# Odd layer: output projection of six heads under the last head pair, with weights and gate prepared earlier

## The chip, the cores and the metric

One Trainium2 chip, one of its cores. The metric is the device time of one execution in microseconds (us). The engines are TensorE (PE; its weight loads are PEld), VectorE (DVE), ScalarE (ACT), GpSimd (POOL) and SyncE (SP), which issues the DMA transfers here.

## The reference, cut to what matters

Two layers run over 512 latent tokens (and, in the even layer, 256 context tokens) of width 1024. Layer 0 has a mixer of delta-rule and retention heads; layer 1, the odd one, has differential attention with 8 heads. Each layer has a mixer and a convolutional feed-forward net; each adds its gated result to the scaled stream and normalizes.

```python
def diff_mix(q, k, v, lam):
    s = jnp.einsum('cbhqd,cbhkd->cbhqk', q, k).astype(jnp.float32) * DIFF_HD ** -0.5
    p = jax.nn.softmax(s, -1)
    a = p[0] - lam * p[1]
    return jnp.einsum('bhqk,bhkd->bhqd', a.astype(v.dtype), v)
...
    def finish(o):
        o = rms_norm(o) * subln_w.astype(f32) * (1.0 - lambda_init)
        return (merge_heads(o).astype(w_out.dtype) @ w_out).astype(h.dtype)
```

The mixer's result y (512x1024) goes into layer_norm(alpha * x + gate * y), with alpha the DeepNorm constant; x is itself the normalized output of the stage before, times ln_g plus ln_b. A gate is a row of 1024 numbers. A matrix product in float32 is computed as three products of high and low parts: a tile is split into a rounded high part (hi) and the rest (lo), and hi*hi, hi*lo and lo*hi are added in PSUM.

## The kernel before, in words

Tokens stand in four tiles of 128 (t = 0 to 3). A weight unit is 256 columns of a 1024-row matrix: `unit` (L174) loads 1 MB into a tile `raw`, multiplies it by a gate row on POOL where one is given (L185), and `split` (L139) writes the high part on ACT (L147, tiles `whi`) and the low part on DVE or POOL (L148, `wlo`); `lo_engs` says which, "v" or "g".

`odd_mixer` (L1540) goes through the 8 heads in four pairs. `attend` (L1649) computes one head tile by tile: scores `sc` on PE, their maximum on DVE (L1663), exp on ACT (L1666), the difference of the two softmaxes on DVE (L1674), transposes and the product with the values on PE (`aT_ps`), copies (L1682), the head's output into `oall` (L1686) and its square sum (L1687). After four tiles the head's norm runs on DVE: a Newton iteration on 128x4 values (L1693, L127 to L136) and four scalings of `oall` (L1696). Between two tiles `attend` yields, and the loop over the pairs takes a few steps of a generator `fill`. In pairs 0 to 2 `fill` is `project` (L1604), which makes keys, queries and values of the next pair; its key and query tiles pass a rotary step (`rope`: products on DVE at L1577 and L1581, sum on POOL at L1583), transposes on PE (`oT_ps`) and evictions on ACT and DVE (L1591 to L1595).

In the last pair (pr == 3) `fill` is `sums` (L1708). At its start the four units of the output matrix are issued: 0 and 1 unscaled and split on DVE, 2 and 3 multiplied by the gate and split on POOL. `sums` transposes a head (`to_y`, L1700: `yT_ps` on PE, high part on ACT at L1705, low part on DVE at L1706) and accumulates its product with units 0 and 1, columns 0 to 511, for the token tiles 0 and 1, which hold the two PSUM banks of the pool `pj`. After the attention come tiles 2 and 3, heads 6 and 7 and then `out_proj_ln` (L1299): the stream is loaded and multiplied by ln_g on DVE and added to ln_b on POOL (`load_x`, L1324, L1325, both rows scaled by alpha at L1317), columns 0 to 511 are multiplied by the gate (L1346) and added (L1347), columns 512 to 1023 are computed and added (L1349), the statistics and the normalization follow (L1220 to L1240), and `h_tiles` (L1265) transposes the result and makes the high and low parts `hTh`, `hTl` for the feed-forward net.

The order on each engine is made when the program is built: a scheduler takes instructions by priority, which is the order in the code moved by `priority(offset)` (L155), so that what is marked with `LATE` (200, L47) may fall behind. At run time each engine takes its own list in order and waits where data or a buffer isn't there.

## Time and profile before

| | us |
|---|---|
| median of three runs | 2075.88 (2069.97 to 2078.63) |
| profiled execution, its own time | 2078.59 |
| its span | 2076.8 |
| PE busy | 1944.0 (94%) |
| DVE busy | 1246.6 (60%) |
| POOL busy | 776.1 (37%) |
| ACT busy | 716.3 (34%) |

The share of PE is a mean over the whole program; the part that the change touches lies between about 1500 and 1700 us of the span. All times below count from the start of the span. In rows of the order of time a row gives the start, the busy time, engine, line, operation, output and inputs; the bracket at the end is the idle time of the engine before it and what ended it.

### The profile page before, as it was taken

The page shows a single profiled execution, that of the slowest core. Times are in us where ns is not written, and L with a number is a line of the kernel's source. Part 1 is how long each engine was busy: PE and PEld are TensorE (multiplying, and loading weights), DVE is VectorE, ACT ScalarE, POOL GpSimd, SP SyncE. Part 2 cuts the span into 40 slices and gives each one's busy share as a digit, 9 for nine tenths or more (in the row PEclk, how much of TensorE's full clock was granted, in tenths as well). Part 3 has the DMA queues.
Part 4 walks back from the last instruction along what each step waited for, and adds up shares of the span by engine and source line. Part 5 has one row for each costly group of instructions (what it writes and reads, how often), then busy time and mean ns, then how long its engine had stood idle before and what let it go on. Part 6 is the DMA issues. An engine that isn't in the chain of part 4 may idle for free. (4 is left out here: it accounts for less than half of the span.)

```text
span 2076.8 us, 33472 instructions
## 1 busy us (share of the span) xinstructions
PE 1944.0 (94%) x13766; PEld 1671.6 (80%) x13766; DVE 1246.6 (60%) x2446; ACT 716.3 (34%) x1252; POOL 776.1 (37%) x412
## 2 busy tenths in 40 slices
PE   6989999999899999999999998999997989999997
PEld 4877777778888988888888886989886887888886
DVE  2354645533466685666666558366667687756567
ACT  2331332522334432222222225354554443323221
POOL 1233223222322244554554434122213126766572
PEclk8999999999999999999999999999999999999999
DMA  8546344455614231111111112010102133233221
GB/s 254 176 124 173 113 132 133 139 159 182 188 53 163 82 102 62 61 61 61 62 61 61 61 61 89 21 42 27 56 32 86 68 131 113 83 100 101 82 81 41
DMA packets 195585, 201.33 MB, mean 97 GB/s; under 512 B 21112, under 2 KB 183512, under 8 KB 195432
## 3 DMA queue, kind: packets, MB, share of 16 engines
q1 hardware_dynamic: 194136, 197.57, 30.4%
q8 instruction: 108, 1.77, 0.4%
q10 hardware_dynamic: 1296, 1.62, 0.2%
q14 instruction: 45, 0.37, 0.1%
HBM read 185.89 MB, written 13.27 MB: 96 GB/s over the span
## 5 line engine op out<-in xcount | busy, mean ns | idle before, releaser
L148 POOL TENSOR_TENSOR wlo<-raw,whi 128x2048 fp32r<-128x2048 f32 (+2 forms) x154 | 413.4, 2709 | 482.4 <-ACT whi L147 454.5
L1442 DVE SCALAR_TENSOR_TENSOR ac<-g_ps,fconvT,ac 128x441 f32<-128x441 f32 (+2 forms) x352 | 243.7, 694 | 191.0 <-ACT ac L1431 181.3
L147 ACT CAST whi<-raw 128x2048 fp32r<-128x2048 f32 (+2 forms) x177 | 200.3, 1169 | 379.7 <-PE d_ps L115 162.9
L115 PE MATMUL d_ps<-whi,hh 128*128 128x512 f32 x440 | 176.4, 401 | 11.4 <-DVE gt L1391 6.6
L115 PE MATMUL d_ps<-whi,hl 128*128 128x512 f32 x440 | 172.6, 392 | 0.6 <-DVE hl L148 0.6
L115 PE MATMUL d_ps<-wlo,hh 128*128 128x512 f32 x440 | 173.0, 393 | 0.0
L115 PE MATMUL opj<-whi,hTh 128*128 128x256 f32 x512 | 146.6, 286 | 2.1 <-ACT oq L1594 1.6
L115 PE MATMUL g_ps<-hTl,whi 128*128 128x512 f32 (+1 forms) x384 | 145.1, 378 | 2.9 <-POOL hTl L148 2.9
L115 PE MATMUL opj<-whi,hTl 128*128 128x256 f32 x512 | 145.2, 284 | 0.0
L115 PE MATMUL u_ps<-hTh,whi 128*128 128x512 f32 (+1 forms) x384 | 144.7, 377 | 0.0
L115 PE MATMUL opj<-wlo,hTh 128*128 128x256 f32 x512 | 144.6, 282 | 0.0
L115 PE MATMUL u_ps<-hTh,wlo 128*128 128x512 f32 (+1 forms) x384 | 144.6, 377 | 0.0
L115 PE MATMUL u_ps<-hTl,whi 128*128 128x512 f32 (+1 forms) x384 | 144.6, 376 | 0.0
L115 PE MATMUL g_ps<-hTh,whi 128*128 128x512 f32 (+1 forms) x384 | 144.5, 376 | 0.0
L115 PE MATMUL g_ps<-hTh,wlo 128*128 128x512 f32 (+1 forms) x384 | 144.2, 376 | 0.0
L115 PE MATMUL fpj<-whi,hTh 128*128 128x256 f32 x432 | 127.2, 295 | 5.8 <-DVE kT L550 4.7
L115 PE MATMUL fpj<-wlo,hTh 128*128 128x256 f32 x432 | 127.3, 295 | 0.0
L115 PE MATMUL fpj<-whi,hTl 128*128 128x256 f32 x432 | 126.3, 292 | 0.0
L115 PEld LDWEIGHTS d_ps<-whi,hh 128*128 128x128 f32 x440 | 83.1, 189 | 38.7 <-DVE gt L1391 17.0
L115 PEld LDWEIGHTS opj<-whi,hTh 128*128 128x128 f32 x512 | 97.2, 190 | 4.2 <-ACT oq L1594 2.6
L115 PE MATMUL c_ps<-hTh,wlo 128*128 128x256 f32 x352 | 98.9, 281 | 0.0
L115 PE MATMUL c_ps<-hTh,whi 128*128 128x256 f32 x352 | 98.8, 281 | 0.0
(462 smaller groups left out, 5011.2 us busy)
## 6 DMA issues: line engine op xcount, KB each, us to landing
mraw<-in_mod_w_dram SPq DMA_DIRECT2D x80, 512.0 KB
raw<-in_f_w_gate_dram SPq DMA_DIRECT2D x22, 1024.0 KB
raw<-in_f_w_up_dram SPq DMA_DIRECT2D x22, 1024.0 KB
raw<-in_f_w_down_dram SPq DMA_DIRECT2D x22, 1024.0 KB
raw<-in_o_w_qkv_dram SPq DMA_DIRECT2D x12, 1024.0 KB
raw<-in_e_w_in_dram SPq DMA_DIRECT2D x10, 1024.0 KB
mraw<-in_mod_w_dram SPq DMA_DIRECT2D x32, 256.0 KB
raw<-in_e_w_in_dram SPq DMA_DIRECT2D x12, 512.0 KB
```

Source lines behind the costliest of these rows:

```text
L115: self.nc.tensor.matmul(out, lhsT=lhsT, rhs=rhs, start=start, stop=stop)
L147: self.nc.scalar.copy(h, r)
L148: lo_eng.tensor_sub(l, r, h.bitcast(F32))
L1442: v.scalar_tensor_tensor(out=o, in0=pv[:, r0 + di:r1 + di, c0 + dj:c1 + dj], scalar=cw[(di + 1) * 3 + dj + 1], in1=o, op0=ALU.mult, op1=AL ...
```

## The change

- The gate row is loaded and summed in two halves of 512 columns (`half_gate`): the first in pair 1, the second at the start of the last pair.
- All four output units are multiplied by the gate and split on POOL. Unit 0 is issued in pair 2 after its sixth attention step, units 1 to 3 at the start of the last pair.
- `oall` now lies in the memory of the tile that the layer norm works in. After the heads 0 to 5 have been transposed, all at the start of the last pair, alpha * (x * ln_g + ln_b) is written over their 768 columns; the last 256 columns of it stand in a tile `rest`. The scaling of ln_g and ln_b by alpha is one ACT operation on both rows.
- `early` is the new `fill` of the last pair: the product of heads 0 to 5 for all four token tiles and both halves of the columns (288 of the 384 matmuls), each result added into the stream by DVE. The loop takes two steps of it per attention step, before one.
- After the attention heads 6 and 7 are transposed, their product (96 matmuls) is computed and added tile by tile, and the layer norm follows. The separate product with the gate is gone.
- `out_proj_ln` keeps the even layer's part alone.

```diff
-                def sums(accs, heads, late=0):
-                    for h in heads:
-                        to_y(h)
-                        with self.priority(late):
-                            self.out_part(accs, us[0], h, h == DHEADS - 1)
-                        yield
+                def early(heads):
+
+                    for n in range(2):
+                        for t in range(NLT):
+                            ps = pj.tile([P, 512], F32, tag="wo", name="wo_ps")
+                            with self.priority(LATE):
+                                for h in heads:
+                                    self.out_part([(t, ps)], us[n], h, h == heads[-1])
+                                    if h == heads[len(heads) // 2 - 1]:
+                                        yield
+                                for o, c0, n_ in rest(t, n):
+                                    v.tensor_add(o, ps[:, c0:c0 + n_], o)
+                            yield
...
+                def out_unit():
+                    sl = slice(len(us) * 256, (len(us) + 1) * 256)
+                    us.append(self.unit([w_out[:, sl]], gates[len(us) // 2][:, (len(us) % 2) * 256:][:, :256]))
+
+                def half_gate(pool, n, gb):
+
+                    t = pool.tile([P, 512], F32, name=f"gate{n}")
+                    nc.sync.dma_start(out=t, in_=self.gd[1][0][0][n * 512:(n + 1) * 512].partition_broadcast(P))
+                    nc.sync.dma_start(out=gb, in_=a["mod_b"][1, 2 * D + n * 512:2 * D + (n + 1) * 512]
+                                      .partition_broadcast(P))
+                    g.tensor_add(t, t, gb)
+                    gates.append(t)
+
                 for pr in range(4):
                     cur, nxt = nxt, {}
                     if pr < 3:
                         fill = project(pr + 1, ((4, 0, 2),), nxt)
+                        if pr == 1:
+                            half_gate(cpl, 0, self.rawp.tile([P, 8 * 256], F32, tag="raw", name="raw")[:, :512])
                     else:
                         stp.close()
-                        us = []
-                        self.lo_engs = "v"
-                        for u in range(4):
-                            if u == 2:
-                                self.lo_engs = "g"
-                                gate = self.gate_rows(self.pool(st, "gate1"), 1, 0, 1)[0]
-                                self.wps = [self.pool(st, "wout1", bufs=2)]
-                            sl = slice(u * 256, (u + 1) * 256)
-                            us.append(self.unit([w_out[:, sl]], gate[:, sl] if u > 1 else None))
+                        for h in range(6):
+                            to_y(h)
...
+                        half_gate(gatep, 1, end[:, 0:2, :].rearrange("p t n -> p (t n)"))
+                        out_unit()
+                        rows = self.rawp.tile([P, 8 * 256], F32, tag="raw", name="raw")
+                        for i, r in enumerate(("ln_g", "ln_b")):
+                            nc.sync.dma_start(out=rows[:, i * D:(i + 1) * D], in_=a[r][0, 1].partition_broadcast(P))
+                        s_.activation(rows, rows, AF.Copy, scale=ALPHA)
+                        for t in range(NLT):
+                            for o, c0 in ((oall[:, t, 0:768], 0), (end[:, t, :], 768)):
+                                cs = slice(c0, c0 + o.shape[1])
+                                nc.sync.dma_start(out=o, in_=self.x_src(2, t)[:, cs])
+                                v.tensor_mul(o, o, rows[:, cs])
+                                g.tensor_add(o, o, rows[:, D + c0:D + c0 + o.shape[1]])
+                        self.wps = [self.pool(st, "wout1", bufs=2)]
+                        out_unit()
+                        out_unit()
                         us = [us[:2], us[2:]]
                         self.lo_engs = "g"
-                        accs = [(t, pj.tile([P, 512], F32, tag="wo", name="wo_ps")) for t in range(2)]
-                        fill = sums(accs, range(6), LATE)
+                        fill = early(range(6))
+                    done = 0
...
-                                for _ in range(3 if pr < 3 else 1):
+                                for _ in range(3 if pr < 3 else 2):
                                     next(fill, None)
+                            done += 1
+                            if pr == 2 and done == 6:
+                                out_unit()
                     for _ in fill:
                         pass
+                for h in (6, 7):
+                    to_y(h)
...
+                for grp in ((0, 1), (2, 3)):
+                    sts = {t: self.ln_stats() for t in grp}
+                    for t in grp:
+                        for n in range(2):
+                            ps = po.tile([P, 512], F32, tag="wo", name="wo_ps")
+                            for h in (6, 7):
+                                self.out_part([(t, ps)], us[n], h, h == 7, first=6)
+                            for o, c0, n_ in rest(t, n):
+                                v.tensor_add(acc[t][:, n * 512 + c0:n * 512 + c0 + n_], ps[:, c0:c0 + n_], o)
+                            self.ln_half(acc[t], sts[t], n)
+                        self.ln_tile(acc[t], sts[t], acc[t], None)
+                    with self.priority(100):
+                        self.h_tiles("f1", grp, [acc[t] for t in grp])
```

POOL in pairs 2 and 3, before. L1583 is a rotary sum, L148 a low part of a weight unit, L1198 the sum of the gate row, L185 a gate product, L1325 the sum with ln_b in the tail.

```order
204 L148 TENSOR_TENSOR wlo<-raw,whi 128x2048
205 L1583 TENSOR_TENSOR otok<-otok,ob 128x512 x2
206 L148 TENSOR_TENSOR wlo<-raw,whi 128x2048 x2
207 L1583 TENSOR_TENSOR otok<-otok,ob 128x512 x2
208 L148 TENSOR_TENSOR wlo<-raw,whi 128x2048
209 L1583 TENSOR_TENSOR otok<-otok,ob 128x512 x2
210 L1198 TENSOR_TENSOR gate_15517<-gate_15517,raw 128x1024
211 L185 TENSOR_TENSOR raw<-raw,gate_15517 128x2048 x2
212 L148 TENSOR_TENSOR wlo<-raw,whi 128x2048 x2
213 L1325 TENSOR_TENSOR lx<-lx,lnb 128x1024 x4
```

The same place on POOL, changed. L1557 is the rotary sum (L1583 before), L1718 the sum of the second half gate, L1752 the sum with ln_b.

```order
208 L185 TENSOR_TENSOR raw<-raw,gate_13772 128x2048
209 L1557 TENSOR_TENSOR otok<-otok,ob 128x512 x2
210 L148 TENSOR_TENSOR wlo<-raw,whi 128x2048
211 L185 TENSOR_TENSOR raw<-raw,gate_13772 128x2048
212 L1557 TENSOR_TENSOR otok<-otok,ob 128x512 x2
213 L148 TENSOR_TENSOR wlo<-raw,whi 128x2048 x2
214 L1718 TENSOR_TENSOR gate_15561<-gate_15561,rest 128x512
215 L185 TENSOR_TENSOR raw<-raw,gate_15561 128x2048
216 L1752 TENSOR_TENSOR rest<-rest,raw 128x256 x3
217 L148 TENSOR_TENSOR wlo<-raw,whi 128x2048
218 L1752 TENSOR_TENSOR rest<-rest,raw 128x256
```

The gate product of unit 0 stands ahead of the two key sums of pair 2, that of unit 1 ahead of the two query sums (row 212); the splits of both units follow behind (row 213), and two more gate operations and the residual sums stand among the units of the last pair.

ACT in the second half of pair 2, before: L1591 to L1595 evict queries, L1638 copies values, L1666 is the exp.

```order
732 L1687 ACTIVATE pt,oss<-oall 128x128
733 L1594 ACTIVATE oq<-oT_ps 64x2x256
734 L1595 CAST oq<-oq 64x2x256
735 L1638 COPY ov<-opj 128x512
736 L1666 ACTIVATE sc,oZ<-sc,mx 128x768
737 L1682 COPY aT<-aT_ps 128x512
```

The same place on ACT, changed: L1746 scales both layer-norm rows, L1612 copies values, L1565 to L1569 evict queries, L1640 is the exp.

```order
732 L1565 ACTIVATE oq<-oT_ps 64x2x256
733 L1612 COPY ov<-opj 128x512
734 L1746 ACTIVATE raw<-raw 128x2048
735 L1568 ACTIVATE oq<-oT_ps 64x2x256
736 L1569 CAST oq<-oq 64x2x256
737 L1640 ACTIVATE sc,oZ<-sc,mx 128x768
```

The scaling of the rows stands ahead of an eviction and of an exp; it waits for the transfers of the two rows, which wait for the tile `raw` that unit 0 gives back with its split.

DVE in the first tiles of the last pair, changed: L1670 scales head 5, L1680 is the low part of a transposed head, L1656 and L1660 are copies of the attention, L1751 is the product with ln_g, L1693 the sum of `early`.

```order
1643 L1670 SCALAR_TENSOR_TENSOR oall<-oall,rs_y,sub 128x128 x4
1644 L1751 TENSOR_TENSOR rest<-rest,raw 128x256
1645 L1645 TENSOR_SCALAR nl<-nl,oZ,nlam 128x1
1646 L1648 SCALAR_TENSOR_TENSOR pt<-sc,nl,pt 128x768
1647 L1680 TENSOR_TENSOR hTl<-yT_ps,hTh 128x512
1648 L1656 COPY aT<-aT_ps 128x256
1649 L1751 TENSOR_TENSOR oall<-oall,raw 128x768 x2
1650 L1660 COPY oall<-aT_ps 128x128
1651 L1656 COPY aT<-aT_ps 128x256
1652 L1751 TENSOR_TENSOR oall<-oall,raw 128x768 x2
1653 L1660 COPY oall<-aT_ps 128x128
1655 L1693 TENSOR_TENSOR oall<-wo_ps,oall 128x512
```

The products with ln_g, which before stood in the tail (L1324), stand between the copies of two attention tiles, and the first sum of `early` behind them.

## Rows read from the trace of the kernel before

**Rows 1.** Busy us of each engine (instructions) by stretch; then PE clock, DMA share, GB/s.

```profile
core 0: us, PE busy (x) PEld busy (x) DVE busy (x) ACT busy (x) POOL busy (x), PEclk, DMA share, GB/s
1540.00:1550.00 10.00, 8.60 (x69) 7.99 (x68) 9.04 (x16) 8.21 (x14) 1.29 (x1) 1.00 0.00 1
1580.00:1590.00 10.00, 5.06 (x34) 4.09 (x34) 9.69 (x18) 3.79 (x8) 5.70 (x2) 1.00 0.63 207
1590.00:1600.00 10.00, 4.01 (x17) 3.92 (x18) 7.56 (x11) 5.35 (x7) 6.56 (x2) 0.50 0.00 1
1580.00:1640.00 60.00, 45.06 (x311) 41.09 (x312) 45.22 (x95) 29.19 (x64) 18.05 (x4) 0.89 0.24 79
1640.00:1650.00 10.00, 10.00 (x86) 9.79 (x85) 3.83 (x15) 2.03 (x3) 0.00 (x0) 1.00 0.17 43
1660.00:1670.00 10.00, 4.40 (x38) 4.21 (x37) 10.00 (x6) 0.00 (x0) 7.22 (x3) 0.93 0.00 0
1670.00:1680.00 10.00, 10.00 (x66) 10.00 (x66) 10.00 (x26) 4.33 (x5) 0.00 (x0) 0.73 0.11 30
```

**Rows 2.** PE in order of time: the waits in the last pair and the tail.

```profile
1581.68 0.85 PE L115 MATMUL sc<-ok,oq 128*128 128x512 f32 x3 [2.95 <-ACT pt L1666]
1595.99 0.58 PE L115 MATMUL wo_ps<-whi,hTl 128*128 128x256 f32 x1 [8.94 <-DVE hTl L1706]
1669.59 0.58 PE L115 MATMUL wo_ps<-whi,hTh 128*128 128x256 f32 x1 [5.60 <-DVE lx L1349]
```

**Rows 3.** DVE in order of time, last pair and head 7's scalings.

```profile
1576.26 2.28 DVE L148 TENSOR_TENSOR wlo<-raw,whi 128x2048 fp32r<-128x2048 f32 x1
...
1584.50 4.35 DVE L136 SCALAR_TENSOR_TENSOR rs_y<-rs_w,rs_y 128x4 f32<-128x4 f32 x1
1588.89 5.33 DVE L1696 SCALAR_TENSOR_TENSOR oall<-oall,rs_y,sub 128x128 f32<-128x128 f32 x4
...
1641.71 1.14 DVE L1696 SCALAR_TENSOR_TENSOR oall<-oall,rs_y,sub 128x128 f32<-128x128 f32 x4
```

**Rows 4.** POOL in order of time, from pair 2 to the tail.

```profile
1537.19 1.27 POOL L1583 TENSOR_TENSOR otok<-otok,ob 128x512 f32<-128x512 f32 x1 [4.50 <-DVE rs_w L134]
...
1570.29 2.40 POOL L1198 TENSOR_TENSOR gate<-gate,raw 128x1024 f32<-128x1024 f32 x1 [23.25 <-DMA gate<-gd]
1584.31 8.97 POOL L185 TENSOR_TENSOR raw<-raw,gate 128x2048 f32<-128x2048 f32 x2 [11.61 <-DMA raw<-in_o_w_out_dram]
1596.71 9.08 POOL L148 TENSOR_TENSOR wlo<-raw,whi 128x2048 fp32r<-128x2048 f32 x2 [3.44 <-ACT whi L147]
...
1687.58 1.28 POOL L148 TENSOR_TENSOR hTl<-hf,hTh 128x512 fp32r<-128x512 f32 x1 [2.32 <-ACT hTh L147]
```

**Rows 5.** Lines L1324 and L1325: count, ns least/median/most, first and last start.

```profile
L1324 DVE TENSOR_TENSOR lx<-lx,lng x4: 1211/2308/3440, 1652.9 to 1662.6; 128x1024 f32<-128x1024 f32 x4
...
L1325 POOL TENSOR_TENSOR lx<-lx,lnb x4: 2341/3051/3322, 1654.3 to 1666.0; 128x1024 f32<-128x1024 f32 x4
```

**Rows 6.** Output products on PE that start between 1639 and 1690.

```profile
L115 PE MATMUL wo_ps<-whi,hTl x102: 275/278/415, 1638.7 to 1685.7; 128*128 128x256 f32 x102
L115 PE MATMUL wo_ps<-whi,hTh x101: 276/279/579, 1638.8 to 1685.5; 128*128 128x256 f32 x101
...
L115 PE MATMUL wo_ps<-wlo,hTh x101: 276/278/415, 1639.0 to 1685.6; 128*128 128x256 f32 x101
```

**Rows 7.** ACT in order of time: unit 0's cast, an exp, the first eviction of `h_tiles`.

```profile
1546.35 1.91 ACT L147 CAST whi<-raw 128x2048 fp32r<-128x2048 f32 x1
...
1556.14 0.88 ACT L1666 ACTIVATE sc<-sc,mx 128x768 f32<-128x768 f32 x1 [0.28 <-DVE mx L1663]
...
1680.73 0.56 ACT L1283 ACTIVATE hf<-ln_ps,hb_f,hs_f 128x256 f32<-128x256 f32 x1 [0.69 <-PE ln_ps L119]
```

**Rows 8.** Issue of units 0 and 1; DMA busy tenths 1533 to 1539, 40 slices.

```profile
1500.85 32.23 SPq L181 DMA_DIRECT2D raw<-in_o_w_out_dram  x2
...
DMA  0000094876689999999999999933610020000000
```

**Rows 9.** PE in order of time, the query transposes of pair 2.

```profile
1538.52 0.66 PE L119 MATMUL oT_ps<-ident,otok 128*128 128x128 f32 x4 [0.49 <-POOL otok L1583]
```

More of the change, by code (lines that the diff above doesn't have):

```diff
@@ L1286, in h_tiles, with out_part @@
             self.split(hf, self.hT[0][:, ks, sl], self.hT[1][:, ks, sl], nc.gpsimd if kq % 2 else nc.vector)
-    def out_part(self, accs, units, k, last):
+    def out_part(self, accs, units, k, last, first=0):
         yh, yl = self.hT
@@ L1296, in out_part, with out_proj_ln @@
                     self.mm(ps[:, u * 256:(u + 1) * 256], xi[:, k, ts], wi[:, k, :],
-                            start=(k == 0 and u == 0 and j == 0), stop=(last and u == 1 and j == 2))
-    def out_proj_ln(self, l, w_out, key, src, xh, groups, accp, accs, us, trp, gates=None):
+                            start=(k == first and u == 0 and j == 0), stop=(last and u == 1 and j == 2))
+    def out_proj_ln(self, w_out, key, xh, groups, accp, accs, us, trp):
         nc = self.nc
         with ExitStack() as st:
-            lnp = self.pool(st, f"lnA{l}")
-            pp = accp if l == 0 else self.pool(st, f"ps_wout{l}", bufs=2, space=PSUM)
-            self.ln_pools(st, f"lnA{l}", trp=trp)
+            lnp = self.pool(st, "lnA0")
+            self.ln_pools(st, "lnA0", trp=trp)
@@ L1306, in out_proj_ln @@
             self.lo_engs = "v"
             self.cparts = 2
-            if l == 0:
-                self.wps = [self.pool(st, f"wout{l}", bufs=2, side="right")]
-                us = [us, [self.unit([w_out[:, u * 256:(u + 1) * 256]]) for u in (2, 3)]]
-            if l == 0:
-                gates = self.gate_rows(lnp, l, 0, 2, self.ln2.tile([P, D], F32, tag="gy", bufs=3, name="gy"))
-            else:
-                lng, lnb = self.affine_rows(lnp, 0, 1)
-                for r in (lng, lnb):
-                    nc.scalar.activation(r, r, AF.Copy, scale=ALPHA)
@@ L1319, in load_x @@
-            def load_x(tiles):
-                for t in tiles:
-                    lx[t] = self.ln2.tile([P, D], F32, tag="lx", bufs=4 if l else 2, name="lx")
-                    nc.sync.dma_start(out=lx[t], in_=self.x_src(src, t))
-                    if l:
-                        nc.vector.tensor_mul(lx[t], lx[t], lng)
-                        nc.gpsimd.tensor_add(lx[t], lx[t], lnb)
-            lx = {}
-            if l:
-                load_x((0, 1, 2, 3))
+            self.wps = [self.pool(st, "wout0", bufs=2, side="right")]
@@ L1330, in out_proj_ln @@
+            us = [us, [self.unit([w_out[:, u * 256:(u + 1) * 256]]) for u in (2, 3)]]
+            gates = self.gate_rows(lnp, 0, 0, 2, self.ln2.tile([P, D], F32, tag="gy", bufs=3, name="gy"))
             for grp in groups:
-                if l == 0:
-                    load_x(grp)
-                gy = lx if l else {t: self.ln2.tile([P, D], F32, tag="gy", bufs=3, name="gy") for t in grp}
+                lx = {t: self.ln2.tile([P, D], F32, tag="lx", name="lx") for t in grp}
+                for t in grp:
+                    nc.sync.dma_start(out=lx[t], in_=self.x_src(0, t))
+                gy = {t: self.ln2.tile([P, D], F32, tag="gy", bufs=3, name="gy") for t in grp}
@@ L1339, in out_proj_ln @@
                         else:
-                            ps = pp.tile([P, 512], F32, tag="wo", name="wo_ps")
+                            ps = accp.tile([P, 512], F32, tag="wo", name="wo_ps")
                             for k in range(KT):
@@ new lines, in odd_mixer, with rest @@
+                        gatep = self.pool(st, "gate1")
+                        end = gatep.tile([P, NLT, 256], F32, name="rest")
+                        def rest(t, n):
+                            if n == 0:
+                                return [(oall[:, t, 0:512], 0, 512)]
+                            return [(oall[:, t, 512:768], 0, 256), (end[:, t, :], 256, 256)]
+                        half_gate(gatep, 1, end[:, 0:2, :].rearrange("p t n -> p (t n)"))
+                        out_unit()
```

37 lines of the change are left out of this document (13 added, 24 removed).

## The prediction

> **What bounds the kernel now.** I read the busy time by stretch first, for the last head pair of the odd layer (1580 to 1640 us) and the output product and layer norm behind it (1640 to 1690). Elsewhere TensorE is busy nearly all the time; here it isn't: 45.06 of 60 us, at a mean granted clock of 0.89, and then 4.40 of the ten after 1660 [rows 1]. Next the order of TensorE's work with its waits: one gap of 8.94 us ends with VectorE's yT residual, one of 5.60 with VectorE's add of the residual stream, one of 2.95 with the exp [rows 2]. After the two long gaps the granted clock falls to its lower level, 1.2 GHz: 0.50 in 1590 to 1600, 0.73 on the mean of 1670 to 1680 [rows 1].
>
> VectorE's rows say what made the gaps. A Newton step on 128x4 values takes 4.35 us at 1584.50, and the four scalings of a head's output 5.33 at 1588.89, where the same four take 1.14 for the last head [rows 3]. Beside them GpSimd runs two gate products, 8.97 us from 1584.31 [rows 4]: VectorE ops with two inputs in SBUF stand still until GpSimd's instruction ends, and the yT residual, which doesn't need SBUF twice, is queued behind them. The tail is the same picture: four residual products on VectorE take 1.21 to 3.44 us each and four sums on GpSimd 2.34 to 3.32 [rows 5], each in the other's way. So the limit in this stretch is TensorE's work plus two stalls made by that lock, each followed by a slow clock.
>
> **The change part by part.** *Tail.* Of the 384 products of the output projection 304 start after 1639, the last attention tile [rows 6]. In the changed order 212 do. The 92 others move ahead; at 86 matmuls in 10 us [rows 1], 0.116 us each, the tail loses 10.7 us. The residual's products and sums leave it too, so the gap of 5.60 goes with 2.7 us of slow clock behind it (0.27 of ten us): 8.3 us. What is late next: head 7's norm, from the last tile at about 1639 to 1642.85 (1641.71 + 1.14 [rows 3]), had more than 60 matmuls as cover and now has 33 (3.8 us), with two PSUM adds between its steps: +1.0, at least 0, at most the whole 4. And the first group's transposes, evictions and splits, from 1680.73 [rows 7] to 1688.86 [rows 4], ran among 96 matmuls of the second group; now some 50 of the feed-forward stand between them, 5.8 us for a chain of 8.1: +2.3, from 0 to all 8.1. Tail: -10.7 - 8.3 + 1.0 + 2.3 = -15.7, bounds -19 and -7.
>
> *Second half of pair 2, GpSimd.* Unit 1 of the output weights is requested at 1533.08 (32.23 us after the first) and its transfer keeps the DMA engines busy until about 1537.2 [rows 8]. Its gate product is new and stands ahead of the first rotary sum of the queries, which before ran at 1537.19 [rows 4]. A product takes 4.5 us (half of 8.97), so that sum would end near 1543.3 instead of 1538.46. TensorE's query transposes came 0.49 us after it was free [rows 9], and the scores and projections are queued behind them: +4.8 us. I take it whole, since what is behind in TensorE's queue can't pass; at best the 1.4 us that it was idle in 1540 to 1550 [rows 1] are taken up. The lock adds nothing: VectorE's norm chain that it hits is over before the rotary sum ends. The clock behind a gap of 4.8 us isn't shown: after 2.95 the stretch 1580 to 1590 stays at 1.00, after 5.60 it falls [rows 1, 2]. I take the nearer, 5.60, so +2.5; bounds 0 and 3. Unit 0's product, at about 1505, meets a GpSimd that had nothing else and costs nothing unless its transfer is late; then the two key sums would wait, at most 4.5.
>
> *Pair 2, ScalarE.* The layer-norm rows are scaled in one new op of 128x2048, for which I take the cast of that shape, 1.91 us [rows 7]. The op stands ahead of an exp that ran at 1556.14. Its transfers wait for unit 0's split: cast to 1548.26 [rows 7], split 4.54 on GpSimd (half of 9.08 [rows 4]), 1 MB about 4.3 (1533.08 to 1537.2 and a little [rows 8]), scaling: the exp would start near 1560.3, 4.2 late. TensorE has 33 projection products, 3.8 us, ahead of what needs it: +1.0, bounds 0 and 4.2.
>
> *Pair 3.* TensorE's 45.06 busy us at 0.89 are 40.1 at full clock; with 92 more matmuls 50.8. Five yT and 48 output products now stand ahead of what needs head 5, and wait for no VectorE chain; with three tiles' scores they are some 10.5 us of work. Unit 1's split (4.54), the half gate sum (1.2, half of a whole row's 2.40 [rows 4]) and unit 2's product (4.5) are GpSimd's there. The norm of head 5 starts behind the split, and its last steps meet unit 2's product: I get about 14 us for it against those 10.5, idle 4. Then four 768-wide products on VectorE and four sums on GpSimd alternate among the copies of two attention tiles: 0.9 + 1.8 each (three quarters of the least of [rows 5]), 10.8 us against 7 of TensorE: idle 3.5. What else was idle before stays: 14.9 less 8.94 and less the 1.68 of the 2.95 that lie in the stretch, 4.3. Sum 50.8 + 4 + 3.5 + 4.3 = 62.6, so +2.6. If only the 4.3 stay: -4.9. If all old idle and the slow clock stay and the alternation comes on top: +10.7 + 3.5 = +14.2.
>
> VectorE loses two splits (2.28 [rows 3]) and, in the tail, four gate products and eight adds, and gains 24 adds from PSUM, 12 of them for `early`; they lie under TensorE's work. Unit 0 and 1 are split on GpSimd instead, 4.54 against 2.28, twice [rows 3, 4]; in pair 3 that makes unit 1's low half 2.3 us later, with 15 matmuls or so ahead of it: I cost it at nothing beyond the lock above. The Trainium skill (GPSIMD Engine Reference, section Engine selection) goes further and gives such two-input work to VectorE, as GpSimd is about twice as slow. The two rows have that ratio; by the rule this move alone would cost its 2.3 us, and the sum would be about -2.5. Here neither row says whether TensorE is already there.
>
> Sum: -15.7 + (4.8 + 2.5) + 1.0 + 2.6 = **-4.8 us**. The profiled execution took 2078.6, so 2073.8 in its terms; it lies 2.7 above the median of the runs, 2075.9, hence **2071**. A measurement of this kernel tells about 0.5%, 10 us, from no change.
>
> **The rivals.** *The stalls in pairs 2 and 3 are mostly filled.* For it: TensorE gets 48 output products before it needs head 5, and the gap at 1540 is partly its own. Then pair 2 costs 2, pair 3 gives 4.9: -15.7 + 2 - 4.9, some -18, 2058. Against: the queue order ahead of the rotary sum is fixed.
>
> *GpSimd becomes the bound of pair 3, and it is slower.* Splits, gate sum, products, and eight residual sums stand on it in one row: 4.5 + 1.2 + 4.5 + 4 x 0.6 + 4.5 + 4 x 1.8 + 4.5 + 4.5 = 33.3 us, against 18.05 busy in 1580 to 1640 [rows 1]. If the norm of head 5 is locked out as long as before and the first output sums, which hold both PSUM banks, wait for the residual sums, pair 3 costs +14.2; with pair 2 at 8.3 and the tail at its poor bound, -7, that is +15, 2091; with the tail as forecast +7, 2083. It decides from where pair 3 loses more than 7.4 (15.7 - 8.3). For it: both GpSimd products at 1584 held a two-input VectorE op to their end [rows 3, 4]. Against: TensorE now has work that needs neither.
>
> *The output product isn't what the tail waits for.* With 92 matmuls less the layer-norm chain and the feed-forward's weight splits end last: the tail gives only 7, the rest costs 10.9, +4, 2080.
>
> **How the numbers follow.** Forecast 0.45, filled 0.25, GpSimd's bound 0.17, tail chain 0.13. Faster by over 0.5% (below 2065.5): nearly all of the second and a little of the first, 0.30. Slower by over 0.5% (above 2086): two thirds of the third, 0.11, and 0.03 for the forecast's and the tail chain's worst bounds, 0.14. Within: 0.56. For the range I leave out the far half of the filled case and of GpSimd's: 2056 to 2086.
>
> **What would show it.** TensorE's gap of 8.94 us gone or under 5, no 5.60 gap behind the last attention tile, and about 212 output products there. A new gap of about 5 us at the query transposes of pair 2, right after a gate product on GpSimd, with a lower clock behind it. A ScalarE wait for a transfer before the row scaling. If the first of the new gaps is missing, I am wrong by 7; if pair 3 is longer than before by over 8, GpSimd's rival holds.

## The result and the profile after

The changed kernel is **slower**, by about 1.1%: median 2100.36 us (2095.37 to 2101.1) against 2074.47 for the kernel before, beside which it ran; ratio 1.0109, 95% interval 1.0089 to 1.013, or some 23 us. The forecast was 2071, its range 2056 to 2086. The profiled execution (2095.37, span 2093.6) is the shortest of the four, so about 5 us of the median's growth are in no profile.

Where the time goes is read from five marks: VectorE's copy of a head's output into `oall` for head 1's second tile and for the last tiles of heads 3, 5 and 7, and the first eviction of the feed-forward's `g_ps`. The same marks of the kernel before (DVE and ACT in order of time):

```profile
1399.57 0.29 DVE L1686 COPY oall<-aT_ps 128x128 f32<-128x128 f32 x1 [0.52 <-PE aT_ps L115]
1499.02 0.28 DVE L1686 COPY oall<-aT_ps 128x128 f32<-128x128 f32 x1
1578.46 0.28 DVE L1686 COPY oall<-aT_ps 128x128 f32<-128x128 f32 x1
1638.57 0.29 DVE L1686 COPY oall<-aT_ps 128x128 f32<-128x128 f32 x1 [2.71 <-PE aT_ps L115]
1701.30 0.69 ACT L1431 ACTIVATE ac<-g_ps,fconvT 128x512 f32<-128x512 f32 x1 [1.35 <-PE g_ps L115]
```

and of the changed kernel:

```profile
1399.37 0.29 DVE L1660 COPY oall<-aT_ps 128x128 f32<-128x128 f32 x1 [0.52 <-PE aT_ps L115]
1505.74 0.28 DVE L1660 COPY oall<-aT_ps 128x128 f32<-128x128 f32 x1
1597.02 0.29 DVE L1660 COPY oall<-aT_ps 128x128 f32<-128x128 f32 x1 [1.30 <-PE aT_ps L115]
1669.49 0.29 DVE L1660 COPY oall<-aT_ps 128x128 f32<-128x128 f32 x1 [1.76 <-PE aT_ps L115]
1716.06 0.69 ACT L1405 ACTIVATE ac<-g_ps,fconvT 128x512 f32<-128x512 f32 x1 [1.35 <-PE g_ps L115]
```

The differences give what each stretch grew by: **pair 1 +6.9, pair 2 +11.8, pair 3 +12.4, tail -16.2, the rest +2.1**, together 17.0. The tail gives what was forecast; the pairs take nearly twice as much back. All runs below are read by these marks, since executions already differ by up to 10 us at the first one, where of the change only the half gate's load and sum stand ahead. Such a figure is good to about 1.4 us: a3, b1, b2, c0, c2 and d1 to d3 have the same edit in pair 1, and six of them grew by 1.0 to 1.1 there, b1 and d1 by 2.4 and 2.5, with a granted clock of 0.98 over the pair in place of 1.00.

TensorE in order of time shows the new gaps (idle time in the bracket), from pair 1 to the tail:

```profile
1426.99 1.51 PE L119 MATMUL aT_ps<-ident,pt 128*128 128x128 f32 x6 [4.19 <-DVE pt L1648]
...
1550.36 1.11 PE L119 MATMUL oT_ps<-ident,otok 128*128 128x128 f32 x4 [5.69 <-POOL otok L1557]
1576.37 1.54 PE L119 MATMUL aT_ps<-ident,pt 128*128 128x128 f32 x6 [2.87 <-DVE pt L1648]
...
1615.15 0.44 PE L119 MATMUL yT_ps<-ident,oall 128*128 128x128 f32 x1 [6.20 <-DVE oall L1670]
1620.29 0.48 PE L119 MATMUL yT_ps<-ident,oall 128*128 128x128 f32 x1 [3.81 <-DVE oall L1670]
1633.47 0.51 PE L115 MATMUL wo_ps<-whi,hTh 128*128 128x256 f32 x1 [3.40 <-DVE nl L1644]
1641.23 1.60 PE L115 MATMUL aT_ps<-ov,aT 128*128 128x128 f32 x12 [2.39 <-ACT aT L1656]
...
1702.71 0.39 PE L115 MATMUL g_ps<-hTl,whi 128*128 128x256 f32 x1 [1.55 <-POOL hTl L148]
```

The gaps of 8.94 and 5.60 [rows 2] are gone, and in the tail none is over 1.6. But pair 1 has a new one of over 2 us, pair 2 two, pair 3 four. The busy time by stretch, in the order of [rows 1], with the granted clock third from the end:

```profile
1540.00:1550.00 10.00, 4.67 (x40) 4.47 (x39) 8.10 (x15) 0.41 (x2) 5.40 (x2) 0.91 0.32 107
1550.00:1560.00 10.00, 9.64 (x59) 9.16 (x60) 7.50 (x17) 7.33 (x12) 1.36 (x2) 0.75 0.00 1
1570.00:1580.00 10.00, 7.13 (x43) 6.65 (x43) 2.74 (x5) 5.60 (x8) 0.00 (x0) 0.77 0.00 0
1580.00:1590.00 10.00, 9.93 (x72) 9.42 (x71) 4.63 (x9) 3.95 (x11) 0.00 (x0) 0.88 0.01 2
...
1610.00:1620.00 10.00, 1.34 (x4) 0.58 (x4) 10.00 (x10) 1.90 (x1) 9.25 (x5) 0.65 0.27 79
...
1670.00:1680.00 10.00, 9.83 (x82) 9.47 (x81) 7.21 (x26) 2.68 (x5) 0.00 (x0) 1.00 0.01 2
```

In 1610 to 1620 TensorE works 1.34 us of ten while VectorE and GpSimd are full. GpSimd in order of time says with what:

```profile
1417.68 4.57 POOL L148 TENSOR_TENSOR wlo<-raw,whi 128x2048 fp32r<-128x2048 f32 x1 [27.84 <-ACT whi L147]
...
1544.60 4.49 POOL L185 TENSOR_TENSOR raw<-raw,gate 128x2048 f32<-128x2048 f32 x1 [5.25 <-DMA raw<-in_o_w_out_dram]
1549.05 1.26 POOL L1557 TENSOR_TENSOR otok<-otok,ob 128x512 f32<-128x512 f32 x1
...
1607.87 4.58 POOL L185 TENSOR_TENSOR raw<-raw,gate 128x2048 f32<-128x2048 f32 x1
...
1615.55 4.54 POOL L148 TENSOR_TENSOR wlo<-raw,whi 128x2048 fp32r<-128x2048 f32 x1
```

and VectorE, two steps and four scalings of heads' norms:

```profile
1417.96 4.32 DVE L134 TENSOR_TENSOR rs_w<-rs_y 128x4 f32<-128x4 f32 x1
...
1608.00 4.47 DVE L134 TENSOR_TENSOR rs_w<-rs_y 128x4 f32<-128x4 f32 x1
...
1614.66 5.84 DVE L1670 SCALAR_TENSOR_TENSOR oall<-oall,rs_y,sub 128x128 f32<-128x128 f32 x4
```

Each of the two steps is held until one of these GpSimd operations ends (1422.25 and 1612.45), and the last of the scalings until 1620.09: the lock of [rows 3, 4], now at other places. ScalarE in order of time adds operations that stand at the head of its list and wait, with attention's exps and copies behind them:

```profile
1570.59 1.92 ACT L1746 ACTIVATE raw<-raw 128x2048 f32<-128x2048 f32 x1 [2.78 <-DMA raw<-in_ln_b_dram]
...
1612.48 1.90 ACT L147 CAST whi<-raw 128x2048 fp32r<-128x2048 f32 x1 [6.44 <-POOL raw L185]
...
1638.80 1.90 ACT L147 CAST whi<-raw 128x2048 fp32r<-128x2048 f32 x1 [4.73 <-POOL raw L185]
```

Pair 3 as a whole, from mark to mark, before (first line) and changed:

```profile
1578.46:1638.57 60.11, 43.90 (x301) 39.66 (x300) 45.91 (x95) 29.49 (x64) 18.05 (x4) 0.89 0.24 79
1597.02:1669.49 72.47, 55.21 (x398) 50.75 (x397) 58.34 (x104) 28.35 (x63) 34.27 (x14) 0.91 0.34 109
```

TensorE is idle for 17.3 us of the changed pair and was for 16.2 before: the old gaps are gone, but new waits as long took their place, and the moved work comes on top.

### The profile page after: what moved, and what is told of

The parts are those of the page before. It is cut to its first block, busy times and chain, and to the rows that moved or that the text cites. A ratio compares the mean times of both kernels' runs of the same rounds, so it can differ in the third digit from the quotient of the medians.

```text
span 2093.6 us, 33513 instructions
## 1 busy us (share of the span) xinstructions
PE 1948.3 (93%) x13766; PEld 1673.0 (80%) x13766; DVE 1252.6 (60%) x2460; ACT 715.1 (34%) x1251; POOL 795.9 (38%) x421
## 5 line engine op out<-in xcount | busy, mean ns | idle before, releaser
L148 POOL TENSOR_TENSOR wlo<-raw,whi 128x2048 fp32r<-128x2048 f32 (+2 forms) x156 | 423.0, 2735 | 514.2 <-ACT whi L147 490.6
L115 PE MATMUL d_ps<-whi,hh 128*128 128x512 f32 x440 | 176.3, 401 | 14.3 <-DVE oall L1463 7.3
```

What stands on the lines that cost most here:

```text
L115: self.nc.tensor.matmul(out, lhsT=lhsT, rhs=rhs, start=start, stop=stop)
L148: lo_eng.tensor_sub(l, r, h.bitcast(F32))
```

## The experiments

Two theories. **Waits:** each loss is a new wait, behind an operation of the preparation that stands ahead of attention's own in an engine's list; take that operation away and the loss goes. **Load:** 92 products, 24 sums and nearly twice GpSimd's work (34.27 us in pair 3 against 18.05) are too much for these pairs, whatever the order. Growth against the kernel before in us, between the marks of one profile each; the ratio is that of the runs, which is the whole kernel:

| run | pair 1 | pair 2 | pair 3 | tail | rest | ratio [95%] |
|---|---|---|---|---|---|---|
| the change | 6.9 | 11.8 | 12.4 | -16.2 | 2.1 | 1.0109 [1.0089, 1.013] |
| a1 | 7.2 | 6.5 | 14.3 | -16.3 | 2.1 | 1.0067 [1.0046, 1.0088] |
| a2 | 7.1 | 3.2 | 14.0 | -15.9 | 2.0 | 1.0048 [1.0025, 1.0071] |
| a3 | 1.0 | 9.2 | 14.0 | -16.3 | 2.2 | 1.0044 [1.0018, 1.007] |
| a4 | 7.2 | 3.1 | 11.3 | -16.3 | 2.0 | 1.0038 [1.0016, 1.0061] |
| b1 | 2.4 | 6.5 | 14.2 | -16.0 | 2.2 | 1.0041 [1.0023, 1.0058] |
| b2 | 1.1 | 6.8 | 10.2 | -19.5 | 1.7 | 1.0006 [0.999, 1.0023] |
| b3 | 0.0 | 0.4 | 15.8 | -17.9 | 2.0 | 1.0005 [0.9985, 1.0025] |
| b4 | 0.0 | 0.4 | 15.1 | -16.4 | 3.1 | 1.0009 [0.9991, 1.0027] |
| c0 | 1.1 | 6.4 | 12.9 | -16.8 | 3.0 | 1.0018 [1.0, 1.0037] |
| c2 | 1.0 | 6.0 | 3.1 | -14.0 | -3.6 | 0.9933 [0.9913, 0.9953] |
| c3 | 0.0 | 0.4 | 12.8 | -17.1 | 2.9 | 0.9985 [0.997, 1.0001] |
| c4 | 0.0 | 0.4 | 10.9 | -18.1 | 2.2 | 0.9987 [0.9969, 1.0006] |
| d1 | 2.5 | 6.5 | 5.6 | -11.5 | -3.8 | 0.9982 [0.996, 1.0005] |
| d2 | 1.0 | 6.1 | 10.4 | -15.9 | 1.8 | 1.0029 [1.0009, 1.005] |
| d3 | 1.0 | 5.9 | 3.1 | -18.4 | 3.4 | 0.9973 [0.9951, 0.9995] |
| d4 | 0.0 | 0.4 | 4.7 | -14.2 | 2.0 | 0.9976 [0.9956, 0.9996] |
| d5 | 0.0 | 0.4 | 12.7 | -12.8 | 2.5 | 1.0018 [0.9999, 1.0037] |

### One suspected wait each

**a1**, no row scaling on ScalarE; alpha is applied in the early sum instead:

```diff
-v.tensor_add(o, ps[:, c0:c0 + n_], o)
+v.scalar_tensor_tensor(out=o, in0=o, scalar=ALPHA, in1=ps[:, c0:c0 + n_], op0=ALU.mult, op1=ALU.add)
...
-s_.activation(rows, rows, AF.Copy, scale=ALPHA)
```

> The scaling of the two layer-norm rows on ScalarE is gone; the first sum of the output product takes alpha with it (alpha * stream + product, one VectorE op as before). Theory of waits (the time is lost in single new waits, each at the head of an engine's queue, and each worth its own length with the slow clock behind it): the gap of 2.87 us at 1573 and the slow clock behind it go, the second half of pair 2 is 6 to 9 us shorter, the whole 6 to 9 us shorter than the changed kernel. Rival, theory of load (the last pair holds more work than the engines can pass there; a wait that goes comes back elsewhere): less than 3 us.

Pair 2 grew by 6.5 in place of 11.8, and the gap of 2.87 is gone: the row scaling cost 5.3 us there, a little less than expected. A little over half of it is idle time of TensorE (10.9 us in the changed pair, 8.1 in a1), the rest busy time that is longer at a lower mean clock (0.93 against 0.96).

**a2**, units 0 and 1 without gate (`gates[...] if len(us) > 1 else None`):

> Leaves out the gate product of units 0 and 1, so columns 0 to 511 of the output product are not gated; the half gate of pair 1 is still loaded and summed. GpSimd loses two products of 4.5 us in pair 2 and nothing else. Theory of waits: the gap of 5.69 us at the query transposes goes, with the slow clock behind it; head 5's first copy in pair 2 is 4 to 7 us earlier, the whole 4 to 8 us shorter than the changed kernel. Theory of load: less than 3 us, and the same time is lost in pair 3.

Pair 2 grew by 3.2, and the gap of 5.69 is gone: the two gate products cost 8.6, more than expected; the gap stood behind unit 1's, ahead of the rotary sum. (Together a1 and a2 name 13.9 of 11.8, so some 2 us are counted in both: a2 keeps a gap of 2.82 where the row scaling waits, but its clock is 1.00 all through pair 2. In b3, with both gone, 0.4 is left.)

**a3**, the first half of the gate asked for after the fourth attention step of pair 1 in place of its start:

```diff
-                        if pr == 1:
-                            half_gate(cpl, 0, ...)
...
+                            if pr == 1 and done == 4:
+                                half_gate(cpl, 0, ...)
```

> The half gate of pair 1 is requested after the fourth attention step of that pair and not at its start; ahead of pair 1's end the order on ScalarE is then that of the kernel before. Theory of waits: the gap of 4.19 us at 1422.8 goes, head 3's copies are 6 to 7 us earlier, as before the change, and the whole is 5 to 7 us shorter. Rival: the shift of 6.7 us in pair 1 comes from the transfer and the sum themselves, wherever they stand: it stays, or turns up at another place, and the time is within 2 us of the changed kernel.

Pair 1 grew by 1.0 in place of 6.9, about as expected; of its gap this row is left:

```profile
1420.85 0.85 PE L119 MATMUL aT_ps<-ident,pt 128*128 128x128 f32 x6 [1.66 <-DVE pt L1648]
```

So it was the place of a small load: its `raw` buffer was taken ahead of a projection unit's, that unit's cast and split came later in the lists, and the split (1417.68) met a norm's step (1417.96). **a4**, no unit gated:

> Leaves out the gate product of all four units: the output product is not gated. Against the run that leaves out units 0 and 1 alone, GpSimd loses two more products of 4.5 us, those of the last pair, and ScalarE's casts of units 2 and 3 no longer wait for them. Theory of waits: of the 10 us that TensorE waits for head 5's scalings about half goes (the part behind unit 2's product; unit 2's split still locks VectorE), and the waits of ScalarE's casts (11 us) no longer hold the copies behind them; pair 3 is 5 to 9 us shorter than in the other run, the whole 10 to 16 us shorter than the changed kernel. Theory of load: pair 3 keeps its length within 3 us.

The output product isn't gated at all here. Pair 2 as in a2. Pair 3 keeps 11.3 although GpSimd has two products less, 2.7 below a2 where 5 to 9 were expected; a gap of 8.27 stands there instead, behind a residual product on VectorE that takes 5.07 us beside a split. In a1 to a3, too, pair 3 is 1.6 to 1.9 longer than in the change. Up to here waits hold for pairs 1 and 2, and pair 3 looks like load.

### Two edits together, then other engines

**b1**, a1 and a3 in one kernel:

> No row scaling on ScalarE and the half gate requested after the fourth step of pair 1, together. Each alone came out 8.7 and 13.5 us shorter than the changed kernel (1.0067 and 1.0044 against 1.0109 of the time before). Theory of waits: the two stand in different pairs and add up, 20 to 24 us, so within 4 us of the kernel before. Theory of load: they don't add, and it stays 6 us or more above the kernel before.

Growths of 2.4, 6.5 and 14.2. Between the marks the two gains add up: from 17.0 a1 takes 3.2, a3 4.6 and b1 7.7, and the 9.3 that are left agree with the ratio, some 8.5 us. The expectation failed all the same ("within 4 us of the kernel before"), because it took the single gains from the ratios to the change, whose runs lie 5 us above its profile. **b2**, b1 with the gate products and splits of units 1 to 3 and the residual's sums on VectorE, GpSimd idle in pair 3 (`eng` is VectorE for these units):

> On top of both: the gate products and splits of units 1 to 3 and the residual sums stand on VectorE, so GpSimd has nothing to do in the last pair but the half gate's sum, and unit 1's product no longer stands ahead of the rotary sums. VectorE gets some 17 us more (three splits and three products of 2.3 each, sums 0.4 and 0.9 each). Theory of the lock (in the last pair VectorE's two-input ops wait for GpSimd's; that is what makes it 11 to 14 us longer than before): pair 3 grows by no more than 6 us over the kernel before although VectorE has more work, and the whole is 4 to 10 us shorter than with both alone. Theory of load (VectorE and TensorE have too much there): pair 3 grows by as much or more, and the whole is not shorter.

```diff
-nc.gpsimd.tensor_mul(rv, rv, scale.unsqueeze(1).to_broadcast([P, KT, 256]))
+(eng or nc.gpsimd).tensor_mul(rv, rv, scale.unsqueeze(1).to_broadcast([P, KT, 256]))
...
-self.split(raw, hi, lo, parts=self.cparts)
+self.split(raw, hi, lo, eng, parts=self.cparts)
...
-g.tensor_add(o, o, rows[:, D + c0:D + c0 + o.shape[1]])
+v.tensor_add(o, o, rows[:, D + c0:D + c0 + o.shape[1]])
```

Pair 3 still grew by 10.2, where 6 at most were expected: the lock alone isn't it. TensorE's largest gap, 8.43, ends with a VectorE operation behind a row of preparation:

```profile
1601.36 1.81 DVE L1751 TENSOR_TENSOR oall<-oall,raw 128x768 f32<-128x768 f32 x2
1603.10 2.28 DVE L185 TENSOR_TENSOR raw<-raw,gate 128x2048 f32<-128x2048 f32 x1
1605.30 1.00 DVE L1648 SCALAR_TENSOR_TENSOR pt<-sc,nl,pt 128x768 f32<-128x768 f32 x1
```

Nor did pair 2 gain: it grew by 6.8 (b1 6.5), although unit 1's gate product left GpSimd. The product now stands in VectorE's list, ahead of the copy of a head's output and of the rotary products; VectorE is idle for 4.88 us before it, most likely for the unit's transfer, asked for at 1529.30:

```profile
1534.48 2.29 DVE L185 TENSOR_TENSOR raw<-raw,gate 128x2048 f32<-128x2048 f32 x1 [4.88 <-issue]
```

So the place in the list counts there, and not GpSimd's speed alone.

**b3**, from the change: units 0 and 1 ungated, the gate multiplied onto the sums in PSUM by VectorE, no row scaling, both half gates at the start of pair 3:

> No row scaling; units 0 and 1 are not multiplied by the gate, their products in PSUM are (eight VectorE ops of 0.68, as the kernel before had four); both half gates are loaded at the start of the last pair, so pairs 1 and 2 have no gate work. Theory of waits: pairs 1 and 2 are as long as before within 3 us, pair 3 is still 10 to 14 longer, the tail 15 shorter: from 5 us below the kernel before to the same. Theory of load: pair 3 takes up the time won, 5 us or more above the kernel before.

```diff
+                                if n == 0:
+                                    v.tensor_mul(ps, ps, gates[0])
...
-        if pr == 1:
-            half_gate(cpl, 0, ...)
...
+        half_gate(gatep, 0, ...)
```

Pairs 1 and 2 are free (0.0 and 0.4), pair 3 is at its worst. **b4**, b3 with the residual's sums on VectorE, changes pair 3 by 0.7 only, where 3 to 6 were expected:

> As the run with the gate on the product, and the eight residual sums (ln_b) on VectorE too, which takes GpSimd's part of the alternation in the last pair away: VectorE gets 5 us more, GpSimd 9 us less. Theory of the lock: pair 3 is 3 to 6 us shorter than in that run, since a residual product of 0.9 us no longer waits for a sum of 1.8 or for a split. Theory of load: no shorter, or longer by VectorE's 5 us.

### What costs pair 3

**c0** is b1 without the residual (its loads, products and sums; the early sums become copies), **c2** is b1 without units 2 and 3 (units 0 and 1 stand in for them):

> The changed kernel without the row scaling and with pair 1's half gate requested after its fourth step (as in the run with both edits, whose pair 3 grew by 14.2 us against before), and in pair 3 the residual is left out altogether: no scale and shift rows, no loads of x, no products on VectorE, no sums on GpSimd; the early sums are copied out of PSUM. The output lacks the scaled stream. Preparation theory (what costs pair 3 is the preparation standing in its first attention tiles ahead of attention's own operations): the growth of pair 3 falls by the residual's share, by 5 to 10 us, to 4 to 9. Load theory (92 matmuls and the sums are too much for a pair): it stays at 12 to 15. Lock theory (GpSimd's operations hold VectorE's products): the four sums of 9.17 us are the largest part of GpSimd's work, so it falls too, but what is left is the split units, 8 or more. Whole kernel 5 to 10 us below the run with both edits, so 2070 to 2080 in a session where before is at 2077.

> The same base, and units 2 and 3 of the output weights are never loaded, gated, cast or split; both halves multiply by units 0 and 1, so columns 512 to 1023 of the product are the wrong ones. The residual stays. Preparation theory: the growth of pair 3 falls by the share of two units (two gate products of 4.58 us and splits of 4.5 on GpSimd, two casts that stood 4.73 to 6.44 us at the head of ScalarE's order), by 4 to 9 us, to 5 to 10 of 14.2. Load theory: it stays at 12 to 15.

```diff
-nc.sync.dma_start(out=o, in_=self.x_src(2, t)[:, cs])
-v.tensor_mul(o, o, rows[:, cs])
-g.tensor_add(o, o, rows[:, D + c0:D + c0 + o.shape[1]])
...
-out_unit()
-out_unit()
-us = [us[:2], us[2:]]
+us = [us[:2], us[:2]]
```

(the first three lines in c0, the others in c2). Without the residual 12.9, a miss for the preparation theory: GpSimd's two gate products and two splits now follow one another from 1599.59 to 1617.62, and head 5's scalings wait for them:

```profile
1604.99 13.04 DVE L1670 SCALAR_TENSOR_TENSOR oall<-oall,rs_y,sub 128x128 f32<-128x128 f32 x4
```

Without the units 3.1 of 14.2, less than expected. TensorE still has its 92 more products there (419 matmuls in the pair, 301 before), so TensorE's load isn't it, and the price is in units 2 and 3; whether in GpSimd's load by them (14.1 us in the pair against 33.3 in b1) or in the order, c2 can't tell. **c3** and **c4** are b3 with the residual written one tile per attention step and the units at steps 2 and 4, first at attention's priority, then behind it:

> The computation is whole here. Base: the run whose gate of columns 0 to 511 is put on the sums in PSUM (pair 1 +1.65, pair 2 -1.25, pair 3 +15.8, ratio 1.0005). The residual is now written one tile per step of pair 3's attention, and units 2 and 3 at its second and fourth step, instead of all of it ahead of pair 3. Preparation theory: attention's own operations come earlier in the order, the growth of pair 3 falls to 3 to 10 us, and the kernel is 5 to 12 us below that run, ratio 0.995 to 0.998. If the scheduler draws the preparation together again, as its order shows for part of the products: as that run, 1.000. Load theory: growth of 14 to 16, ratio 1.000.

> As the run with the spread preparation, but the preparation is given the priority that the projections of the earlier pairs have (behind attention's operations). Preparation theory: attention goes first wherever both are ready, growth of pair 3 again 3 to 10 us, ratio 0.994 to 0.998; the early sums may come later and meet the tail, which then costs up to 5 us more. Load theory: growth of 14 to 16, ratio 1.000.

```diff
+if pr == 3 and done < 4:
+    with self.priority(0):
+        residual(done)
+        if done in (1, 3):
+            out_unit()
```

(c4: `priority(100)`.) 12.8 and 10.9 of 15.8: some gain, less than expected. (The +1.65 and -1.25 that c3's expectation gives for b3 are not read by the marks, which give 0.0 and 0.4.) Then units 2 and 3 of b1 part by part: **d1** loads and gate products alone, **d2** the casts as well (the high part stands in for the low one, in place of a split), **d3** the casts without the gate products:

> The run with both edits (pair 3 grew by 14.2 us), and of units 2 and 3 only the loads and the two gate products on GpSimd are left: no cast, no split; both halves multiply by units 0 and 1, so columns 512 to 1023 are wrong. Without units 2 and 3 altogether the growth was 3.1. If the gate products' lock on VectorE is the cost: 9 to 13. If it is the casts at the head of ScalarE's order or the splits: 3 to 5.

> As the run with loads and gate products alone, and the two casts on ScalarE are back, each behind its gate product; no split (the low part is replaced by the high part, so columns 512 to 1023 are wrong). If the casts that wait for GpSimd at the head of ScalarE's order are the cost: growth of pair 3 of 9 to 13, and a wait of 4 to 7 us of ScalarE for GpSimd's gate product stands in the profile. If the splits are: 4 to 7.

> As the run with gates and casts, without the two gate products: the casts of units 2 and 3 wait for their loads alone; no split, no gate on columns 512 to 1023. If the wait for GpSimd is what makes the casts dear: growth of pair 3 of 3 to 6. If ScalarE's 3.8 us of casts or a late load is: 7 to 12.

```diff
-out_unit()
+nc.sync.dma_start(out=rv, in_=w_out[:, sl].rearrange("(k p) n -> p k n", p=P))
+g.tensor_mul(rv, rv, gates[1][...])
+nc.scalar.copy(hi, raw)
```

(d1 without the last line, d3 without the line ahead of it.) ScalarE's casts of units 2 and 3 in d2, where pair 3 grew by 10.4:

```profile
1598.73 1.90 ACT L1726 CAST whi<-raw 128x2048 fp32r<-128x2048 f32 x1 [6.18 <-POOL raw L1723]
1621.12 1.90 ACT L1726 CAST whi<-raw 128x2048 fp32r<-128x2048 f32 x1 [4.72 <-POOL raw L1723]
```

and in d3, where it grew by 3.1, as without the units:

```profile
1589.70 1.91 ACT L1726 CAST whi<-raw 128x2048 fp32r<-128x2048 f32 x1 [0.56 <-DMA raw<-in_o_w_out_dram]
1599.04 1.90 ACT L1726 CAST whi<-raw 128x2048 fp32r<-128x2048 f32 x1 [0.76 <-DMA raw<-in_o_w_out_dram]
```

In pair 3 the casts alone cost nothing; gate products with casts queued behind them cost 7.3 (10.4 - 3.1), and the splits 3.8 more (14.2 - 10.4). How the 7.3 divide between gate product and cast isn't settled: by pair 3 it is 2.5 and 4.8, but d1's tail gave 4.4 less than d2's. With pair 3 and tail together it is 4.9 and 0.4, with the rest as well 4.7 and 6.0.

**d4** is c4 with every gate product on the sums, none on GpSimd; **d5** the same with the preparation in one block ahead of pair 3, as in the change:

```diff
-us.append(self.unit([w_out[:, sl]], gates[1][...] if len(us) > 1 else None))
+us.append(self.unit([w_out[:, sl]], None))
...
-if n == 0:
-    v.tensor_mul(ps, ps, gates[0])
+v.tensor_mul(ps, ps, gates[n])
```

> The computation is whole here. As the run with the preparation behind attention (pair 3 grew by 10.9, ratio 0.9987), and now no unit of the output weights is gated: each sum in PSUM is multiplied by the gate, 8 products of 0.69 us early and 8 in the tail on VectorE, where 4 and 4 stood. GpSimd loses two operations of 4.5 us in pair 3. If the casts' wait for the gate products is the cost: growth of pair 3 of 3 to 7, ratio 0.994 to 0.997. If the splits' lock or the load as a whole is: 10 to 14 and a tail longer by 1 to 3, ratio 0.999 to 1.002.

> The computation is whole here. All gate products on the sums in PSUM, as in the run that came out at 0.9976 (pair 3 grew by 4.7 us), but the residual and units 2 and 3 stand in one block ahead of pair 3, as in the change. If the casts' wait for the gate products was all of pair 3's cost: growth 4 to 6, ratio 0.997. If the splits of units 2 and 3 also meet the residual's products on VectorE (as where no unit was gated, growth 11.3): 9 to 12, ratio 0.999 to 1.002.

d4: 4.7, and the ratio is 0.9976 [0.9956, 0.9996]; that is half of the 0.5% that the prediction takes a measurement to tell from no change, so it isn't called faster here. d5: 12.7. The two run the same operations in another order, so 8.0 us of pair 3 are the order's and not the load's, GpSimd's included (d4, then d5):

```profile
1583.11:1647.89 64.78, 55.36 (x419) 51.69 (x418) 56.45 (x111) 27.83 (x63) 25.73 (x13) 0.95 0.40 131
1574.33:1647.09 72.76, 55.22 (x408) 51.43 (x407) 63.66 (x111) 28.26 (x63) 25.79 (x13) 0.88 0.36 116
```

In d5's block VectorE's residual products stand ahead of attention and are locked by the splits, and TensorE waits for what is behind them:

```profile
1600.83 4.77 DVE L1751 TENSOR_TENSOR rest<-rest,raw 128x256 f32<-128x256 f32 x1
```

```profile
1612.40 1.54 PE L119 MATMUL aT_ps<-ident,pt 128*128 128x128 f32 x6 [9.05 <-DVE pt L1648]
```

So pair 3 has several waits that stand in for one another. The rows name three: VectorE's scalings of head 5 behind GpSimd's gate products and splits (10.0 us in the change); attention's copies behind ScalarE's casts, which wait for the gate products (2.39); and attention's operations behind VectorE's residual products, which wait for the splits (9.05 in d5, 8.27 in a4). That fits the 10 to 13 us that were left when one was taken away: without the gate products the third is there (a4, d5), without the splits the first, smaller, and the second (d2: 5.97 and 3.84), without the residual the first, 10.6 in three gaps (c0). b2 has none of GpSimd's, but the same preparation in VectorE's own list. c2 and d3, without gate products and splits of units 2 and 3, and d4, without gate products and with the residual behind attention, are nearly free; d4 keeps a wait of 5.62 for head 5's scalings, behind unit 1's split. d1, with gate products that no cast waits for, lies between. How the change's own 12.4 divide among the three no run shows.

## Why the prediction was wrong

- *Tail, -15.7:* right. It measured -16.2, the gap of 5.60 and the slow clock behind it are gone (1.00 in 1670 to 1680), and 210 output products start after the last attention tile (212 were forecast, in a count that takes in those just running).
- *Pair 1:* the step is missing. "The change part by part" prices the half gate nowhere, though it is a load on SP's queue, and takes a buffer, ahead of a projection unit. The pair grew by 6.9 us, and 5.9 of them go with the load's place (a3).
- *Second half of pair 2, GpSimd, 4.8 + 2.5:* right in mechanism and nearly in size, 8.6 by a2, which takes away unit 0's product too; the gap was 5.69, the clock behind it 0.75. The lock hit a norm's step as well (4.40 at 1544.70), whose chain was not over before the rotary sum, as I had it, but 1.4 us after; TensorE waited for the rotary sum.
- *Pair 2, ScalarE, +1.0 (0 to 4.2):* mis-sized, 5.3 by a1. ScalarE stood 2.78 us for the transfer and 1.92 in the scaling, 4.7 together where 4.2 were forecast (the terms given for it add up to 1559.0 and 2.9, not to 1560.3 and 4.2); but TensorE had run out of products at 1573.50 and waited 2.87, so the "33 projection products ahead of what needs it" covered 1.8 and not 3.8. The low clock was put at nothing: it is 0.77 and 0.88 in the two stretches of ten shown, and nearly half of the 5.3 is busy time that it made longer.
- *Pair 3, +2.6 (to 14.2):* 12.4, near the far bound. The work in it was right: 55.21 busy us at a clock of 0.91 are some 50 at full clock, where 50.8 were forecast, and the 48 output products and five heads' transposes ran ahead of head 5, until 1608.95. The alternation (idle 3.5, where its own 10.8 less 7 is 3.8) came out at 3.40, and what else was idle (4.3) at 3.9, the copies behind a cast, which the prediction doesn't name, among it. Two terms failed. Head 5's norm was to keep TensorE idle for 4; the `yT` transposes waited 6.20 + 3.81 us for its scalings, since unit 2's gate product held a step of the norm (4.47), as forecast, and then unit 2's split the scalings, which no term has: the norm ran from 1597.78 to 1620.50, 22.7 us, where about 14 were forecast. And the slow clock was put at nothing without a reason: all work was priced at full clock, 50.8, and took 55.2. These two, 6.0 and 4.4, less the 0.5 that the other terms came out shorter, make up the 9.8 that were missing. Whether unit 1's split on GpSimd is worth nothing beyond the lock, as the prediction has it, no run shows by itself.
- *The rest:* +2.1 behind the tail was forecast as nothing. No run explains it; in c2 and d1, which have no casts of units 2 and 3, it turned to -3.6 and -3.8, and in d3, with the casts alone, it stayed at 3.4.

Of the rivals "GpSimd becomes the bound of pair 3" was nearest: it decides from 7.4 lost in pair 3, and 12.4 were; its 2083 lacks pair 1, as the forecast does. Its mechanism is half right, since with GpSimd idle (b2) 10.2 were lost still. b2 also answers the Trainium skill's advice (GPSIMD Engine Reference, section Engine selection) to give two-input products to VectorE: from b1 to b2 pair 3 and the tail gained 7.5 together and pair 2 nothing; three products, three splits and the sums moved, so this can't be set beside the 2.3 that the prediction works out by that rule for one split. The Trainium skill has a caution as well (Perfetto Trace Analysis, section Optimizing Scalar/DVE Operations): moving work between these two engines might not help, because they share a port. Here it did help, by 4.0 of pair 3's 14.2 us, and 10.2 stayed in VectorE's own list.

The sum with measured terms: 6.9 + 11.8 + 12.4 - 16.2 + 2.1 = 17.0. Some 5 us by which the other runs of the changed kernel lie above the profiled one stay open.

## What to carry to other kernels

Preparation that is moved under other work isn't hidden by a busy TensorE; each of its operations takes a place in an in-order list, and what it waits for is then waited for by everything behind it. Price a moved step at its place in the new list, with the producer it waits for (a transfer, GpSimd) and the operations queued behind, on each engine and on each buffer that it takes, in every stage that it is moved past. When one wait is taken away and the time stays, look for a second one that stood behind it before calling it load.

## What was not expected of the hardware

A gap of 2.95 us left TensorE's clock at its upper level in the kernel before [rows 1, 2]; in the changed one a gap of 2.87 is followed by 0.77 and 0.88. In a2 and a3 gaps of 2.82 and 3.11 at the same place left it at 1.00 too, while in the kernel before a gap of 1.91 that ends at 1634.15 is followed by 0.50 in 1634.5 to 1637.9. Nor was TensorE idler ahead of the gap in the changed kernel: it worked 3.49 of the 3.50 us from 1570, and before 3.40 of the 3.73 from 1575. What tells them apart stays open, and the size of a gap alone doesn't price it.
